# Reordering a fused gMLP, attention and PEER block: exponentials, scaling, weight splits and gathers

## The chip, the core and the metric

The kernel runs on one core of a Trainium2 chip. The metric is the device time of one execution in microseconds (us), from runs that were timed on the chip. TensorE is called PE below, VectorE DVE, ScalarE ACT, GpSimd POOL and SyncE SP, as the profile does. POOL and SP and ACT also issue DMAs; each engine works through its own queue in order.

## What is computed

One layer of a streaming encoder, for 512 tokens of width 1024, all in float32:

```python
xn   = rms_norm(x, ln_mix_g);  proj = xn @ w_in            # 1024 x 2560
a    = gmlp_spatial_gating(proj[..., :512], proj[..., 512:1024], ...)
b    = banded_chunk_attention(q, k, v, ...)                # 8 heads of 64
x    = x + concat([a, b]) @ w_out
# PEER on y = rms_norm(x): 8 heads, 16 of 128 x 128 experts each
q    = y @ w_query;  sc = q . sub_keys                     # two halves of 128 keys per head
s_top, i_top = top_k(sc, 16)                               # per half
best, pos = top_k(all sums of the two halves, 16)          # 16 experts per head and token
g    = softmax(best)
h    = gelu(expert_u[eidx] . y)
out  = x + sum(g * h * expert_v[eidx])
```

There are 16384 experts, each with a row of 1024 in `expert_u` and in `expert_v`.

## The kernel before

**Two ways to the experts.** Of the four tiles of 128 tokens, three (and of these all tokens but the last 64 for the first product) are computed densely: all 16384 experts' products with the tokens, scaled with a matrix of gates that is zero for experts that were not chosen. The experts are cut into 128 blocks of 128 (`NB`), two blocks make a chunk c (`BC`, 64 chunks). The remaining tokens gather the chosen rows from memory by indirect DMAs of POOL.

**Split weights.** A float32 product is made of three products of a high and a low half: `load_split` loads 512 KB (`raw`, three buffers, issued by SP), ACT copies the high half (`hi`, L155, five buffers), and DVE or POOL subtracts it for the low half (`lo`, L156, five buffers). `mm3` (L194 to L196) multiplies hi by hi, hi by lo and lo by hi. In the first stage `load_pieces` does the same with lines L143 and L144; there a piece is split as a whole, but for the first piece, which comes in two DMAs and is split in two.

**The stages in time.** (1) Norm, the first product with `w_in`, attention and gate, up to about 245 us. (2) Routing of the three dense tiles (queries, keys, top 16) with some blocks of the first expert product filled in. (3) The gate stage, some 430 to 590 us, which builds the matrix of gates. (4) The second product over the chunks c, to the end.

**The gate stage** runs over n, eight tokens a step (48 steps and two more). Its order on PE, DVE, ACT and POOL is the program's order. In a step, POOL multiplies the one-hot digits `hb` and `lb` to `bm` (L968, three buffers), PE multiplies `bm` and `am` of step n - 2 to the gates (L985, sixteen instructions), ACT copies them out (L988), DVE makes `am` (L976, three buffers) and a row product of gathered rows (L665, `dots_early`), POOL issues one gather of a row of `expert_u` for 128 tokens and slots (L655, `gather_early`, six buffers), DVE makes digits for a later step, PE does a share of the first expert product (`multiply_some`, results in `pu`, two buffers, activated by ACT's gelu at L719), and one split of the next weights is put in the queues: `split_next`, on DVE, each fourth on POOL, while fewer than `HELD` = 2 tiles are ready.

**The second product**, chunk c: load and split two blocks of `expert_v`, scale the activations with the gates (`act` times `gc`, L1168 on DVE), take their high half (`wh`, L1169 on ACT) and low half (`wl`, L1170 on DVE), and multiply on PE (L1202). The gates `gc` come back from memory in groups of four chunks, in two buffers. As long as c + 25 < 64, the chunk is followed by two tiles of the first expert product for chunk c + 25, each with its gelu. Between these, DVE handles the gathered rows (L1128, L1139). Only PE's order is the program's here; the other queues are ordered by a planner, which weighs priorities and expected times, and an instruction is kept behind another one of the same engine where `tc.issue_after` or `queued_behind` says so. `done` holds the newest gelu, `marked` the newest `am` or `wl`.

For every third chunk (`ROUTE`) up to c = 21, `route_gathered` routes one head of the gathered tokens: top 16, candidates, choice, and the softmax with its exponential on ACT (L804), which stands between a subtraction (L803) and a sum (L806) on DVE. Exponential and gelu need different tables on ACT, so ACT_TABLE_LOAD instructions stand ahead of them.

Of the kernel before, what the change touches and what calls it, by code (L numbers as in the profile page):

```python
# [8 lines left out]
F32 = mybir.dt.float32  # L9
# [5 lines left out]
ALU = mybir.AluOpType  # L15
# [52 lines left out]
AHEAD = 25  # L68
LAST = 2
HELD = 2  # L70
SOME = 15
FILL = (0, 1, 2, 3, 4, 4, 3, 3)
DELAY = 6
# [20 lines left out]
def hybrid_block(tc, x, ln1, w_in, gng, wsT, bsb, qkg, bias, w_out, ln2, wq, skT, uT, ud, vd, out):  # L94
    nc = tc.nc
    ctx = ExitStack()
    with ctx:
# [35 lines left out]
        def load_pieces(src, n, b):  # L133

            raw, hi, lo = big("raw", F32, RAW), big("hi", F32R, HI), big("lo", F32R, LO)
            m = 1024 // n
            cs = [slice(i * m, (i + 1) * m) for i in range(n)]
            for i in range(n):
                nc.sync.dma_start(raw[:, cs[i]] if n > 1 else raw.rearrange("p (a b) -> p a b", b=b),
                                  src[:, i, :] if n > 1 else src)  # L140

            def split(i=0):
                nc.scalar.activation(hi[:, cs[i]], raw[:, cs[i]], AF.Copy)  # L143
                nc.vector.tensor_tensor(lo[:, cs[i]], raw[:, cs[i]], hi[:, cs[i]].bitcast(F32), op=ALU.subtract)  # L144
            return [v.rearrange("p (a b) -> p a b", b=b) for v in (hi, lo)], split

        def load_split(src, eng=nc.vector, **dims):
# [29 lines left out]
        class Pieces:  # L177
# [5 lines left out]
                self.parts[j] = load_pieces(self.w[2 * j * P:2 * (j + 1) * P, self.c * CW:(self.c + 1) * CW]  # L183
                                            .rearrange("(k p) n -> p k n", p=P), 1 if j else self.first, CW)

            def split(self, j, i=0):
                self.parts[j][1](i)

            def __call__(self, k, cols=slice(0, CW)):
                return tuple(v[:, k % 2, cols] for v in self.parts[k // 2][0])  # L190
# [83 lines left out]
        with tc.tile_pool(name="prea", bufs=1, reuse_waits="tile") as prea:  # L274
# [33 lines left out]
            def scale_of(t):  # L308
                r = rs1[:, t:t + 1]
                nc.vector.tensor_scalar(r, r, 1.0 / D, EPS, op0=ALU.mult, op1=ALU.add)  # L310
                nc.scalar.activation(r, r, AF.Sqrt)
                return nc.vector.reciprocal(r, r)
# [6 lines left out]
            with tc.manual_schedule(engines=first):  # L319
# [17 lines left out]
                def product(t, ps, ks):  # L337
                    tok = slice(t * P, (t + 1) * P)
                    for k in ks:
                        mm3(ps, (xh[:, k, tok], xl[:, k, tok]), w_at(k), k == 0, k == KT - 1)  # L340
# [2 lines left out]
                halves(0, 1, xg[1])  # L343
                w_at.split(0, 1)
                product(0, ps0, range(2))
                w_at.split(1)
                product(0, ps0, range(2, 4))
                scale_of(0)
                w_at.load(3)
                w_at.split(2)  # L350
                product(0, ps0, range(4, 6))
                pss = turned(1)
                w_at.split(3)

                def next_halves(t, pss):
                    xg = [gained(ps, j) for j, ps in enumerate(pss)]
# [439 lines left out]
                                          mask[:, i, :, :, None].to_broadcast([P, n, TOPK, m]), other)  # L796
            nc.vector.tensor_copy(to, tree[:, :, :, 0])

        def softmax(pool, best, n):

            full = [P, n, TOPK]
            ex = pool.tile(full, F32, name="ex")
            nc.vector.tensor_tensor(ex, best, best[:, :, 0:1].to_broadcast(full), op=ALU.subtract)  # L803
            nc.scalar.activation(ex, ex, AF.Exp)  # L804
            zs = pool.tile([P, n], F32, name="zs")
            nc.vector.reduce_sum(zs, ex, axis=AX.X)  # L806
            nc.vector.reciprocal(zs, zs)
            nc.vector.tensor_tensor(best, ex, zs[:, :, None].to_broadcast(full), op=ALU.mult)
# [207 lines left out]
        with tc.manual_schedule(engines=engines):  # L1016
# [5 lines left out]
            for n in range(steps + LEAD):  # L1022
# [16 lines left out]
                    ready_early(NH - 3 + n)  # L1039
                if n:  # L1040
                    dots_early(LAGE, 1)
                if 1 < n < own - 7 and n % 4 != 1:
                    gather_early(1, gat, ROWA)
                if t + 1 < ND:
                    if c == per - 5:
# [26 lines left out]
                left = (AHEAD - LAST) * BC * KT - split * KT + made  # L1072
                some = -(-left // (steps + LEAD - n))
                multiply_some(some)
                if n > 1 and split < (AHEAD - LAST) * BC + HELD and len(ready) < HELD:
                    split_next(nc.vector if split % 4 else nc.gpsimd)
            while ready or open_tile:
                if split == AHEAD * BC and not weights:
# [28 lines left out]
        def route_gathered(b):  # L1107

            n = NH // PARTS
            sc = (scores.pop(b) if b in scores else scores_of(b, nc.sync))[0]  # L1110
            top, pos = keys(ep, n)
            for h in range(n):
                for p2 in range(2):
                    best_keys(ep, top, pos, h, p2, sc[:, h, p2, :])
            hs = slice(b * n * TOPK, (b + 1) * n * TOPK)
            best, to = (x[:, 0, hs].rearrange("p (h k) -> p h k", k=TOPK) for x in (gate, eidx))
            mask = ep.tile([P, 6 * n * TOPK], U32, name="mask", tag="mask", bufs=1)
            tree = ep.tile([P, D], F32, name="tree", tag="row", bufs=ROW)
            choose(ep, pairs(ep, top, pos, n, behind=list(routed if b else done)), n, best, to, mask,
                   tree[:, 0:n * TOPK * 32].rearrange("p (h k m) -> p h k m", h=n, k=TOPK))  # L1120
            softmax(ep, best, n)
            nc.vector.tensor_copy(eint[:, hs], eidx[:, 0, hs])

        def gather_u(j):
            row = ep.tile([P, D], F32, name="row", tag="row", bufs=ROW)
# [32 lines left out]
        def second_product(c, between):  # L1158
# [2 lines left out]
            act = acts.pop(c)  # L1161
            wh = ep.tile([P, BC, NDT], F32R, name="wh", tag="wh", bufs=2)
            wl = ep.tile([P, BC, NDT], F32R, name="wl", tag="wl", bufs=2)
            with queued_behind(marked if c < GB // BC else []):
                for b in range(BC):
                    bb = (c * BC + b) % GB
                    av = act[:, b, :].rearrange("p (n t) -> p n t", t=TG)
                    nc.vector.tensor_tensor(av, av, gc[:, 0:NDU // TG, bb, :], op=ALU.mult)  # L1168
# [46 lines left out]
        with tc.manual_schedule(engines={mybir.EngineType.PE}):  # L1215
            for c in range(NCHK):
# [7 lines left out]
                    if c:  # L1224
                        ahead()
                if c % ROUTE == 0 and c < PARTS * ROUTE:
                    route_gathered(c // ROUTE)
                passed = c + 1 + min(c + 1, NCHK - AHEAD)
                with tc.issue_after(mark.ins if hasattr(mark, "ins") else mark):
                    gather_some(min(total, total * max(0, passed - DELAY) // (weight - SLACK - DELAY))  # L1230
# [55 lines left out]
```

## Time and profile before

| | |
|---|---|
| time, median of 3 runs | 1425.32 us (1420.27 to 1426.73) |
| the profiled execution's own time | 1418.47 us |
| its span, first to last instruction | 1416.7 us |
| mean granted clock of PE | 0.998 |
| PE busy | 1387.3 us, 98% of the span |
| DVE busy | 1157.5 us, 82% |
| POOL busy | 699.0 us, 49% |
| ACT busy | 610.5 us, 43% |
| HBM traffic | 363.34 MB read, 31.46 MB written |

A row of a timeline gives start, duration, engine, line, operation, tiles (out <- in) and shapes; in brackets stands the time that the engine was idle before it and what ended that. A row of the waits gives the total, the number of waits and the longest. A row of the windows gives the stretch and its length, busy time of PE, its weight load, DVE, ACT and POOL with the number of instructions, then the granted clock, the DMA engines' share and GB/s. Busy shares are means over stages with different limits, so the waits of the engine that is nearly always busy are read place by place.

### The profile page before, as it was taken

The page shows a single profiled execution, that of the slowest core. Times are in us where ns is not written, and L with a number is a line of the kernel's source. Part 1 is how long each engine was busy: PE and PEld are TensorE (multiplying, and loading weights), DVE is VectorE, ACT ScalarE, POOL GpSimd, SP SyncE. Part 2 cuts the span into 40 slices and gives each one's busy share as a digit, 9 for nine tenths or more (in the row PEclk, how much of TensorE's full clock was granted, in tenths as well). Part 3 has the DMA queues.
Part 4 walks back from the last instruction along what each step waited for, and adds up shares of the span by engine and source line. Part 5 has one row for each costly group of instructions (what it writes and reads, how often), then busy time and mean ns, then how long its engine had stood idle before and what let it go on. Part 6 is the DMA issues. An engine that isn't in the chain of part 4 may idle for free.

```text
span 1416.7 us, 21660 instructions
## 1 busy us (share of the span) xinstructions
PE 1387.3 (98%) x7838; PEld 1224.6 (86%) x7838; DVE 1157.5 (82%) x2505; ACT 610.5 (43%) x955; POOL 699.0 (49%) x486
## 2 busy tenths in 40 slices
PE   9999999999998999989999999999999999999998
PEld 7887788899998989978998889889889989888877
DVE  5537845898999998679999999889989887688883
ACT  5447635443443545444434443334433334333331
POOL 0002104778779898325554556455565553345430
PEclk9999999999999999999999999999999999999999
DMA  4452326667667999978999899999999998888882
GB/s 165 133 193 75 105 75 193 209 214 275 235 229 257 330 352 272 292 265 332 334 331 356 328 352 347 355 376 353 386 375 365 347 364 311 288 332 326 335 335 89
DMA packets 164330, 396.24 MB, mean 280 GB/s; under 512 B 12880, under 2 KB 75232, under 8 KB 162176
## 3 DMA queue, kind: packets, MB, share of 16 engines
q1 hardware_dynamic: 64640, 194.14, 37.9%
q0 software_dynamic: 48176, 173.46, 33.2%
q10 hardware_dynamic: 51408, 27.27, 6.5%
q8 instruction: 61, 1.00, 0.3%
q14 instruction: 45, 0.37, 0.1%
HBM read 363.34 MB, written 31.46 MB: 279 GB/s over the span
## 4 chain that ended last, share of the span: by engine, by line
PE 31%; DVE 12%; DMA 8%; issue 4%; ACT 1%; POOL 0%; SPq 0%; DVEq 0%; ACTq 0%; POOLq 0%
PE pa L1202 13%; PE px L1202 6%; PE pu L194 4%; PE pu L196 4%; PE pu L195 4%; DMA gc<-gd 4%; DVE lo L156 3%; DVE row L1128 2%; DVE acc L1139 2%; DMA row<-in_ud,eint 2%; DVE act L1168 1%; DMA raw<-in_uT 1%; DMA row<-in_vd,eint 1%; DVE wl L1170 1%; DMA raw<-in_vd 1%
## 5 line engine op out<-in xcount | busy, mean ns | idle before, releaser
L155 ACT ACTIVATE hi<-raw 128x1024 fp32r<-128x1024 f32 x296 | 312.9, 1059 | 470.9 <-DMA raw<-in_vd 156.6
L156 DVE TENSOR_TENSOR lo<-raw,hi 128x1024 fp32r<-128x1024 f32 x244 | 307.0, 1259 | 72.1 <-ACT hi L155 71.6
L1126 POOL DMA_INDIRECT row<-in_ud,eint x128 | 198.5, 1551 | 159.6 <-DVE acc L1139 107.2
L1137 POOL DMA_INDIRECT row<-in_vd,eint x128 | 179.7, 1404 | 192.0 <-DVE row L1128 131.5
L194 PE MATMUL pu<-xch,hi 128*128 128x320 f32 x784 | 247.5, 316 | 8.6 <-ACT act L719 8.6
L196 PE MATMUL pu<-xch,lo 128*128 128x320 f32 x784 | 242.8, 310 | 0.0
L195 PE MATMUL pu<-xcl,hi 128*128 128x320 f32 x784 | 242.7, 310 | 0.0
L1202 PE MATMUL pa<-lo,wh 128*128 128x512 f32 x512 | 199.7, 390 | 0.0
L1202 PE MATMUL pa<-hi,wh 128*128 128x512 f32 x512 | 199.4, 389 | 0.0
L156 POOL TENSOR_TENSOR lo<-raw,hi 128x1024 fp32r<-128x1024 f32 x52 | 124.1, 2401 | 116.3 <-ACT hi L155 115.3
L1139 DVE SCALAR_TENSOR_TENSOR acc<-row,hw,acc 128x1024 f32<-128x1024 f32 x128 | 165.6, 1294 | 2.4 <-DMA row<-in_vd,eint 2.0
L1128 DVE SCALAR_TENSOR_TENSOR row<-row,xb 128x1024 f32<-128x1024 f32 x128 | 155.9, 1220 | 12.0 <-DMA row<-in_ud,eint 12.0
L1202 PE MATMUL pa<-hi,wl 128*128 128x512 f32 x512 | 158.4, 389 | 0.0
L194 PEld LDWEIGHTS pu<-xch,hi 128*128 128x128 f32 x784 | 148.0, 189 | 12.0 <-ACT act L719 10.4
L195 PEld LDWEIGHTS pu<-xcl,hi 128*128 128x128 f32 x784 | 148.1, 189 | 1.4
L196 PEld LDWEIGHTS pu<-xch,lo 128*128 128x128 f32 x784 | 147.8, 188 | 0.2 <-DVE lo L156 0.2
L1202 PEld LDWEIGHTS pa<-hi,wh 128*128 128x128 f32 x512 | 96.1, 188 | 20.6
L1202 PEld LDWEIGHTS pa<-hi,wl 128*128 128x128 f32 x512 | 96.1, 188 | 20.2
L1202 PEld LDWEIGHTS pa<-lo,wh 128*128 128x128 f32 x512 | 96.1, 188 | 20.2
L985 PE MATMUL pa<-bm,am 128*128 128x128 f32 x768 | 96.3, 279 | 7.9 <-DVE am L976 5.0
L985 PEld LDWEIGHTS pa<-bm,am 128*128 128x128 f32 x768 | 92.3, 194 | 10.8 <-issue 5.5
L1202 PE MATMUL px<-hi,wh 128*128 128x512 f32 x256 | 100.1, 391 | 0.6 <-ACT hi L155 0.6
(236 smaller groups left out, 2634.1 us busy)
## 6 DMA issues: line engine op xcount, KB each, us to landing
raw<-in_uT SPq DMA_DIRECT2D x128, 512.0 KB, 5.6
raw<-in_vd SPq DMA_DIRECT2D x128, 512.0 KB, 6.1
gd<-gst ACTq DMA_DIRECT2D x24, 1024.0 KB, 8.9
gc<-gd SPq DMA_DIRECT2D x15, 1280.0 KB, 9.8
raw<-in_w_in SPq DMA_DIRECT2D x19, 512.0 KB, 4.6
raw<-in_wq SPq DMA_DIRECT2D x16, 512.0 KB, 4.5
raw<-in_w_out SPq DMA_DIRECT2D x8, 512.0 KB, 3.7
gc<-gd SPq DMA_DIRECT2D x15, 256.0 KB, 10.3
```

What stands on the lines that cost most here:

```text
L155: top = nc.scalar.activation(hi, raw, AF.Copy)
L156: ins = eng.tensor_tensor(lo, raw, hi.bitcast(F32), op=ALU.subtract)
L194: nc.tensor.matmul(ps, lh[0], rh[0], start=first, stop=False)
L195: nc.tensor.matmul(ps, lh[0], rh[1], start=False, stop=False)
L196: nc.tensor.matmul(ps, lh[1], rh[0], start=False, stop=last)
L985: nc.tensor.matmul(ps[:, i * P:(i + 1) * P], am[:, 4 * q + i, :], bm[:, 4 * q + i, :], start=True, stop=True)
L1126: nc.gpsimd.indirect_dma_start(out=row, out_offset=None, in_=ud, in_offset=bass.IndirectOffsetOnAxis(ap=eint[:, j:j + 1], axis=0))
L1128: nc.vector.scalar_tensor_tensor(row, row, 1.0, xb0, op0=ALU.mult, op1=ALU.mult, accum_out=hw[:, j:j + 1])
L1137: nc.gpsimd.indirect_dma_start(out=row, out_offset=None, in_=vd, in_offset=bass.IndirectOffsetOnAxis(ap=eint[:, j:j + 1], axis=0))
L1139: nc.vector.scalar_tensor_tensor(acc0, row, hw[:, j:j + 1], acc0, op0=ALU.mult, op1=ALU.add)
L1168: nc.vector.tensor_tensor(av, av, gc[:, 0:NDU // TG, bb, :], op=ALU.mult)
L1202: nc.tensor.matmul(accs[t][half], (wh, wh, wl)[k][:, b, tok], w[b][k % 2][:, ds_], start=first and k == 0, stop=last and k == 2)
```

## The change

Four things are reordered; no arithmetic is added or taken away.

- **Loop exponentials behind gelus.** `softmax` is cut in two. `route_gathered` ends with the subtraction (`shifted`) and returns; exponential, sum, reciprocal and product follow two chunks later (c = 2, 5, 8, ...), the exponential behind the newest gelu on ACT.
- **Scaling behind weights.** The scaling products (L1168) of every chunk are queued behind the newest `wl` on DVE, where that held for the first four chunks alone.
- **The gate stage's begin.** Up to n = 8 (`EASY`) a split is put in the queues only at even n. Gathers are issued from n = 6 on, but for n = 9, 17 and 25; before it was from n = 2 on, but for n = 5, 9, 13, ..., 29.
- **First weights by halves.** Pieces 1, 2 and 3 of the first weights are split in two halves each, and the scale of the first tile of tokens comes behind the split of piece 2, not ahead of it.

```diff
+EASY = 8
...
-            def split(i=0):
-                nc.scalar.activation(hi[:, cs[i]], raw[:, cs[i]], AF.Copy)
-                nc.vector.tensor_tensor(lo[:, cs[i]], raw[:, cs[i]], hi[:, cs[i]].bitcast(F32), op=ALU.subtract)
+            def split(i, n):
+                c = slice(i * (1024 // n), (i + 1) * (1024 // n))
+                nc.scalar.activation(hi[:, c], raw[:, c], AF.Copy)
+                nc.vector.tensor_tensor(lo[:, c], raw[:, c], hi[:, c].bitcast(F32), op=ALU.subtract)
...
-                w_at.split(1)
+                w_at.split(1, 0)
+                w_at.split(1, 1)
                 product(0, ps0, range(2, 4))
+                w_at.load(3)
+                w_at.split(2, 0)
+                w_at.split(2, 1)
                 scale_of(0)
-                w_at.load(3)
-                w_at.split(2)
                 product(0, ps0, range(4, 6))
                 pss = turned(1)
-                w_at.split(3)
+                w_at.split(3, 0)
+                w_at.split(3, 1)
...
-        def softmax(pool, best, n):
+        def shifted(pool, best, n):
 
             full = [P, n, TOPK]
             ex = pool.tile(full, F32, name="ex")
             nc.vector.tensor_tensor(ex, best, best[:, :, 0:1].to_broadcast(full), op=ALU.subtract)
-            nc.scalar.activation(ex, ex, AF.Exp)
+            return ex
+
+        def softmax(pool, best, n, ex=None, behind=()):
+
+            full = [P, n, TOPK]
+            if ex is None:
+                ex = shifted(pool, best, n)
+            with queued_behind(behind):
+                nc.scalar.activation(ex, ex, AF.Exp)
...
-                if 1 < n < own - 7 and n % 4 != 1:
+                if EASY - 3 < n < own - 7 and n % 8 != 1:
                     gather_early(1, gat, ROWA)
...
-                if n > 1 and split < (AHEAD - LAST) * BC + HELD and len(ready) < HELD:
+                if n > 1 and split < (AHEAD - LAST) * BC + HELD and len(ready) < HELD and (n > EASY or n % 2 == 0):
                     split_next(nc.vector if split % 4 else nc.gpsimd)
...
-            softmax(ep, best, n)
             nc.vector.tensor_copy(eint[:, hs], eidx[:, 0, hs])
+            return best, n, shifted(ep, best, n)
...
-            with queued_behind(marked if c < GB // BC else []):
+            with queued_behind(marked):
...
-                    route_gathered(c // ROUTE)
+                    chosen = route_gathered(c // ROUTE)
+                if c % ROUTE == ROUTE - 1 and c < PARTS * ROUTE:
+                    softmax(ep, *chosen, behind=list(done))
```

More of the change, by code (lines that the diff above doesn't have):

```diff
@@ L184, in load, with split @@
                                             .rearrange("(k p) n -> p k n", p=P), 1 if j else self.first, CW)
-            def split(self, j, i=0):
-                self.parts[j][1](i)
+            def split(self, j, i=0, n=2):
+                self.parts[j][1](i, n)
             def __call__(self, k, cols=slice(0, CW)):
```

## The prediction

> **What bounds the kernel now.** I read the page's engine list first, then the waits of TensorE (PE), then the windows with the granted clock, then the timelines around each wait. Times below are microseconds from the start of the span; n is a step of the gate stage, c a chunk of the second product.
>
> ```profile
> PE 1387.3 (98%) x7838; PEld 1224.6 (86%) x7838; DVE 1157.5 (82%) x2505; ACT 610.5 (43%) x955; POOL 699.0 (49%) x486
> ```
>
> PE is busy for 98% of the span, so nothing off PE counts unless PE waits for it. The waits are a short list (total, times, longest):
>
> ```profile
> PE pu L194 <- ACT act L719: 9.7, 6, 4.7
> PE pa L985 <- DVE am L976: 5.0, 2, 4.7
> PE pa L985 <- POOL bm L968: 2.8, 8, 1.1
> PE px L1202 <- DVE wl L1170: 1.6, 1, 1.6
> PE pu L195 <- DVE lo L144: 1.3, 3, 0.8
> ```
>
> The four parts of the change aim at these rows in this order: exponentials at the first, the gate stage at the second and third, scaling at the fourth, first weights at the fifth. Together they hold 20.4. Two single waits of 4.7 cost more than they show: in the windows behind them the granted clock (first number after the five engines) is 0.66.
>
> ```profile
> 458.00:463.00 5.00, 4.71 (x25) 4.74 (x26) 4.97 (x10) 1.17 (x2) 3.23 (x3) 0.66 1.00 352
> ...
> 632.00:637.00 5.00, 5.00 (x25) 5.00 (x25) 1.04 (x1) 0.00 (x0) 1.32 (x2) 0.66 0.99 408
> ```
>
> A third of 5.0 is 1.7 lost each time. So 20.4 + 3.4 = 23.8 is the most that this change can bring.
>
> **Part 1, exponentials behind gelus (-7).** ScalarE (ACT) works its queue in order. Before, the routing of a head puts its exponential (L804) wherever the planner finds it ready; the gelu (L719) that empties an accumulator of the first product stands behind it, and PE waits for that accumulator.
>
> ```profile
> 627.81 0.21 ACT L804 ACTIVATE ex<-ex 128x16 f32<-128x16 f32 x1 [3.15 <-DVE ex L803]
> 627.93 1.99 ACT L155 ACTIVATE hi<-raw 128x1024 fp32r<-128x1024 f32 x2
> 629.94 1.28 ACT L719 ACT_TABLE_LOAD   x1
> 631.23 0.77 ACT L719 ACTIVATE act<-pu 128x320 f32<-128x320 f32 x2
> ```
>
> ```profile
> 631.72 0.41 PE L194 MATMUL pu<-xch,hi 128*128 128x320 f32 x1 [4.71 <-ACT act L719]
> ```
>
> ```profile
> 752.91 0.42 PE L194 MATMUL pu<-xch,hi 128*128 128x320 f32 x1 [0.78 <-ACT act L719]
> ```
>
> ```profile
> 800.07 0.41 PE L194 MATMUL pu<-xch,hi 128*128 128x320 f32 x1 [0.92 <-ACT act L719]
> ```
>
> ```profile
> 848.25 0.41 PE L194 MATMUL pu<-xch,hi 128*128 128x320 f32 x1 [2.13 <-ACT act L719]
> ```
>
> ```profile
> 797.10 0.22 ACT L804 ACTIVATE ex<-ex 128x16 f32<-128x16 f32 x1 [4.19 <-DVE ex L803]
> ```
>
> ```profile
> 846.46 1.28 ACT L719 ACT_TABLE_LOAD   x1
> ```
>
> After it, the subtraction (L803) stays in the routing at c = 0, 3, 6, ... and the exponential is queued two chunks later, behind the gelu just issued: its input is long there, and the longest stretch to the next gelu follows. At 631 the wait for DVE, the exponential and one table load, 3.15 + 0.21 + 1.28 = 4.64, leave the queue ahead of the gelu; of 4.71 nearly nothing stays, and the 1.7 of slow clock go too: 6.3. At 752 a load is 1.28 against a wait of 0.78, at 800 the 4.19 alone exceed 0.92: both go, 1.7. At 848 only the reload, 1.28, stands right before the gelu: 1.3 of 2.13 go. Sum 9.3. Against it: the table is still reloaded ahead of the next gelu, eight times 1.28. Eight exponentials gave four waits in their bad place, and no more than one in five should be caught in the new one: 1.6 x 1.28 = 2.0. I take -7; ends: the four waits and the clock, -10.2, and +3 if the reloads are caught where VectorE (DVE) is late (next rival).
>
> The Trainium skill, page "ScalarE: Activation LUTs", section "What ACT_TABLE_LOAD costs", puts a switch of table sets at about 2.66, a load and as much again to drain. The trace disagrees in these rows: 629.94 + 1.28 is 631.22, and the gelu starts at 631.23. By the page's figure two caught reloads would cost 4 and this part would bring 5.
>
> **Part 2, scaling behind weights (-1.6).** From c = 4 on, the products act x gc (L1168) were free to go ahead of the weights' low halves (L1170) of earlier chunks. DVE then stood idle until the gates had landed:
>
> ```profile
> DVE act L1168 <- DMA gc<-gd: 40.3, 12, 5.3
> ```
>
> ```profile
> 1349.71 2.10 DVE L1168 TENSOR_TENSOR act<-act,gc 128x320 f32<-128x320 f32 x5 [5.31 <-DMA gc<-gd]
> ```
>
> Only once did that reach PE: the 1.6 for L1170 in the list above, right behind this row. Queued behind the wl of the chunk before, L1168 comes about a chunk before its use; its two products take 2 x 0.42 = 0.84 (2.10 / 5), so wl of the same chunk is not late. Behind the waiting L1168 stood everything on DVE, gathers' row work included; that is freed, but PE has no other wait there. Ends: -1.8 and +0.5. Late next: nothing on PE until the end.
>
> **Part 3, the gate stage (0).** Up to n = 8 the splits of weights come at even n alone, and gathers start at n = 6 and skip n = 9, 17, 25, where they started at n = 2 and skipped 5, 9, 13, ..., 29. The stall removed:
>
> ```profile
> 451.95 5.07 DVE L156 TENSOR_TENSOR lo<-raw,hi 128x1024 fp32r<-128x1024 f32 x1
> ```
>
> ```profile
> 451.68 2.38 POOL L156 TENSOR_TENSOR lo<-raw,hi 128x1024 fp32r<-128x1024 f32 x1
> 454.02 1.91 POOL L968 TENSOR_TENSOR bm<-hb,lb 128x1024 f32<-128x1024 f32 x1
> ```
>
> ```profile
> 458.29 3.59 PE L985 MATMUL pa<-bm,am 128*128 128x128 f32 x16 [4.74 <-DVE am L976]
> ```
>
> A lo on DVE that mostly takes 1.22 took 5.07: it ended 1.1 after POOL's back-to-back lo and bm had ended at 455.93. The Trainium skill, page "SBUF — State Buffer", section "Who interferes with whom", states that a DVE instruction with two SBUF inputs and a GpSimd one that reads SBUF exclude each other, whoever starts first. The trace agrees, 5.07 against 1.22. It also speaks against this change: bm after bm with no gather between them is just what a lo has to sit out.
>
> With splits at n = 2, 4, 6, 8 the lo of n = 5 is gone from this place and the stall with its clock, 4.74 + 1.7 = 6.4, should go. What comes instead: at n = 2 the lo started beside a gather and held up bm of n = 3 (2.67 long); without the gather that bm starts 1.0 earlier and comes first:
>
> ```profile
> 441.66 1.23 DVE L156 TENSOR_TENSOR lo<-raw,hi 128x1024 fp32r<-128x1024 f32 x1 [1.14 <-ACT hi L155]
> ```
>
> ```profile
> 440.93 1.02 POOL L655 DMA_INDIRECT rowe<-in_ud,eui  x1 [0.27 <-POOL eui L671]
> 442.01 2.67 POOL L968 TENSOR_TENSOR bm<-hb,lb 128x1024 f32<-128x1024 f32 x1
> ```
>
> so this lo waits about 1.0 (or 3.0, should the next bm get in as well), and PE needs it at once. PE's tiles don't run out otherwise: a step takes three of a tile's eight k there, so a split every 2.7 steps is enough. A split's hi on ACT and the next load on SP, which waits for its raw buffer, move along with it. Then POOL. Its ledger to 536.65:
>
> ```profile
> L968 POOL TENSOR_TENSOR bm<-hb,lb 128x1024 f32<-128x1024 f32 x33 | 65.5, 1993 | 5.4 <-DVE lb L957 4.3 <-PE pa L985 0.6
> L655 POOL DMA_INDIRECT rowe<-in_ud,eui x22 | 25.7, 1169 | 3.6 <-issue 2.7 <-POOL eui L671 0.3 <-PE pa L985 0.2
> ```
>
> ```profile
> 433.20:536.65 103.45, 96.98 (x755) 94.44 (x754) 100.11 (x148) 50.36 (x83) 95.44 (x61) 0.98 0.96 311
> ```
>
> ```profile
> 504.20 2.05 PE L985 MATMUL pa<-bm,am 128*128 128x128 f32 x16 [0.17 <-POOL bm L968]
> ...
> 507.31 2.05 PE L985 MATMUL pa<-bm,am 128*128 128x128 f32 x16 [0.18 <-POOL bm L968]
> ```
>
> ```profile
> 539.42 1.95 PE L985 MATMUL pa<-bm,am 128*128 128x128 f32 x16
> 542.09 1.95 PE L985 MATMUL pa<-bm,am 128*128 128x128 f32 x16
> ```
>
> POOL is at work for 95.44 of 103.45. With gathers a step takes 507.31 - 504.20 = 3.11, POOL's pace; without, 2.67, PE's own. The same 22 gathers are issued, now in n = 6 to 30: three move from n = 2, 3, 4, where the buffers of bm (three) leave POOL time, to n = 13, 21, 29, where it sets the pace. Each costs (25.7 + 3.6) / 22 = 1.33: 4.0. POOL's lo (2.38) moves from n = 5, inside the stall, to n = 8. So -6.4 + 1.0 + 4.0 + 2.4 = +1.0; a part of the time won at n = 7 does help POOL too, and I take 0. DVE's rows move with the gathers and are hidden under POOL's pace. Ends: -5.4 (POOL keeps up) and +2.9.
>
> **Part 4, first weights by halves (-0.3).**
>
> ```profile
> 13.36 1.06 ACT L143 ACTIVATE hi<-raw 128x1024 fp32r<-128x1024 f32 x1 [1.54 <-DMA raw<-in_w_in]
> ```
>
> ```profile
> 14.45 1.23 DVE L144 TENSOR_TENSOR lo<-raw,hi 128x1024 fp32r<-128x1024 f32 x1 [1.37 <-ACT hi L143]
> ```
>
> ```profile
> 7.43 0.68 DVE L144 TENSOR_TENSOR lo<-raw,hi 128x512 fp32r<-128x512 f32 x1
> ```
>
> The first lo of a piece is there half a split earlier (1.23 - 0.68 = 0.55 on DVE, about 0.5 of the 1.06 on ACT), and part of the 1.3 that PE waits goes. But the last piece waits for its DMA until 13.36 in either kernel; by halves its lo start 0.5 sooner and take 2 x 0.68 - 1.23 = 0.13 more, so the work for the next tile of tokens behind them is 0.3 to 0.4 earlier. The scale moved behind the split is used only after the whole product, and on SP the loads keep their order. Ends: -1.3 and +0.4.
>
> **Sum.** -7 - 1.6 + 0 - 0.3 = -8.9. The profiled execution took 1418.47 (span 1416.7), so 1409.6; the median of the three runs is 6.85 higher, 1425.32, and 1416.4 is the forecast for a median.
>
> **The rivals.**
>
> *POOL keeps up.* The gate stage keeps most of its 6.4. For it: 8 of 103.45 idle on POOL. Against: 6.4 of its work (4.0 + 2.4) lands where PE waits for it. Then -8.9 - 5 = -13.9: 1411.4.
>
> *The loop's gain comes back as new waits.* Between 640 and 850 DVE is at work for 202.61 of 210:
>
> ```profile
> 640.00:850.00 210.00, 206.16 (x1128) 184.98 (x1127) 202.61 (x468) 94.08 (x139) 113.16 (x78) 1.00 0.91 338
> ```
>
> PE's waits there are 0.78 + 0.92 + 2.13 = 3.83, and DVE has 7.4 free; if lateness on DVE and not the exponential holds the gelus, the three waits return in other places, and of the first one (6.4 with its clock) some half goes. Then -3 - 1.6 - 0.3 = -4.9: 1420.4, no change that can be told. For it: 96% on DVE, and 848, where the exponential stood ahead of a wait for DMA. Against: the 4.19 and 3.15 are the exponentials' own.
>
> *Slower: DVE waits for a late exponential.* The sum (L806) follows the exponential on DVE, whose queue is in order. Behind the gelu, the exponential is as late as PE and ACT are; if the planner puts L806 close behind, DVE stands, and with 7.4 free in 210, eight waits w cost PE 8w less about 7. From w = 2 it decides: 16 - 7 = 9 lost; the 7 of part 1 are lost too. Then -8.9 + 7 + 9 = +7.1: 1432.4. For it: the 12 waits of L1168 show that DVE does stand in such places. Against: L806 has no urgency and can stand anywhere within three chunks.
>
> **How the numbers follow.** My sum 0.45, POOL keeps up 0.15, gain comes back 0.28, slower 0.12. A measurement tells about 0.5%, 7.1. My sum lies 1.8 beyond that and is within some 4 either way: of its 0.45, 0.30 are faster and 0.15 the same. With 0.15 and a little of the third: faster 0.48, same 0.40 (0.15 + 0.25), slower 0.12. The range reaches from POOL keeping up with 2.4 of the 3.2 that part 1 can bring beyond -7 (1411.4 - 2.4 = 1409.0) to 1428, short of the slower case; my own sum alone 1412 to 1421.
>
> **What would show it.** Right: no wait for L719 over 1 between 600 and 860, each L804 right behind an L719; the waits of L1168 for gc near 0; no clock of 0.66 behind 458 or 632; steps of 3.1 in the gate stage from about n = 10 to n = 30, with PE waiting for bm. Wrong: gelus still late with nothing but hi ahead of them, DVE idle before L806, a new gap at n = 3, or gate steps of 2.8 under gathers.

## The result, and the profile after

The changed kernel takes 1411.62 us (median of 7 runs, 1410.74 to 1413.98), the kernel before, in the same sessions, 1419.00 (7 runs, 1416.26 to 1426.73). The ratio is 0.9934 with a 95% interval of 0.9916 to 0.9951: faster by 0.5 to 0.8%. The profiled execution took 1410.74, with a span of 1409.0, against 1418.47 and 1416.7.

The busy line and the first waits of PE after, then the one wait for `gc` that is left on DVE (total, times, longest):

```profile
PE 1386.7 (98%) x7838; PEld 1224.6 (87%) x7838; DVE 1154.3 (82%) x2508; ACT 612.0 (43%) x960; POOL 673.0 (48%) x486
```

```profile
PE pa L998 <- POOL bm L981: 4.2, 8, 1.2
PE pu L196 <- ACT act L724: 3.0, 3, 2.0
PE pa L998 <- DVE ff L889: 1.9, 2, 1.5
PE pa L998 <- DVE am L989: 1.7, 2, 1.4
```

```profile
DVE act L1181 <- DMA gc<-gd: 4.5, 1, 4.5
```

Lines have moved by 2 to 13: L719 is L724 now, L985 is L998, L968 is L981, L1168 is L1181. The wait for the gelu fell from 9.7 to 3.0, that for `am` from 5.0 to 1.7; that for `bm` rose from 2.8 to 4.2, and `ff` came in new. The wait for `wl` is gone.

**The loop.** The timeline of ACT around the longest wait that is left, PE's row for it, and two windows behind (the first number after the five engines is the granted clock):

```profile
627.18 2.00 ACT L157 ACTIVATE hi<-raw 128x1024 fp32r<-128x1024 f32 x2 [1.83 <-issue]
629.09 0.74 ACT L724 ACTIVATE act<-pu 128x320 f32<-128x320 f32 x2
```

```profile
629.56 0.41 PE L196 MATMUL pu<-xch,hi 128*128 128x320 f32 x1 [2.02 <-ACT act L724]
...
765.93 0.42 PE L196 MATMUL pu<-xch,hi 128*128 128x320 f32 x1 [0.73 <-ACT act L724]
```

```profile
458.00:463.00 5.00, 5.00 (x44) 5.00 (x43) 4.97 (x9) 2.75 (x5) 4.17 (x3) 1.00 0.96 280
...
631.00:634.50 3.50, 3.50 (x15) 3.50 (x15) 1.32 (x2) 0.00 (x0) 3.10 (x2) 0.51 0.98 413
```

No exponential and no table load stands ahead of this gelu any more, and still PE waits 2.02: two `hi`'s stand there, and the first began at 627.18, after 1.83 of idle time for which the profile names no releaser. The slow clock behind it has stayed, 0.49 x 3.5 = 1.7. At 752, 800 and 848 PE waits no longer; 0.73 at 766 is new.

**The gate stage.** The clock behind 458 is full, the stall is gone, and the stage is not shorter. The starts of the first and the last step's products, before and after:

```profile
438.10 1.95 PE L985 MATMUL pa<-bm,am 128*128 128x128 f32 x16
...
581.81 1.95 PE L985 MATMUL pa<-bm,am 128*128 128x128 f32 x16
```

```profile
438.62 1.95 PE L998 MATMUL pa<-bm,am 128*128 128x128 f32 x16
...
582.53 1.95 PE L998 MATMUL pa<-bm,am 128*128 128x128 f32 x16
```

581.81 - 438.10 = 143.71 before, 582.53 - 438.62 = 143.91 after. What was won at 458 went in five waits, two of them for POOL's `bm` and three for DVE:

```profile
444.31 0.42 PE L198 MATMUL pu<-xch,lo 128*128 128x320 f32 x1 [0.78 <-DVE lo L158]
...
487.30 0.35 PE L998 MATMUL pa<-bm,am 128*128 128x128 f32 x1 [1.40 <-DVE am L989]
...
499.47 0.38 PE L998 MATMUL pa<-bm,am 128*128 128x128 f32 x1 [1.20 <-POOL bm L981]
512.68 0.38 PE L998 MATMUL pa<-bm,am 128*128 128x128 f32 x1 [0.99 <-POOL bm L981]
526.02 0.35 PE L998 MATMUL pa<-bm,am 128*128 128x128 f32 x1 [1.54 <-DVE ff L889]
```

A step of 3.11 does not tell by itself whose pace it is. Before, the products that start at 466.15 and 469.26 have nine matmuls of the first product between them and no wait, so 3.11 is PE's own pace there. Those at 504.20 and 507.31 have six and a wait for `bm`. After the change PE's rows wait for `bm` from 499.47 to 518.89 and once more at 549.99; only there does POOL set the pace.

### The profile page after: what moved, and what is told of

It reads as the page before. It is cut to its first block, busy times and chain, and to the rows that moved or that the text cites. A ratio compares the mean times of both kernels' runs of the same rounds, so it can differ in the third digit from the quotient of the medians.

```text
span 1409.0 us, 21692 instructions
## 1 busy us (share of the span) xinstructions
PE 1386.7 (98%) x7838; PEld 1224.6 (87%) x7838; DVE 1154.3 (82%) x2508; ACT 612.0 (43%) x960; POOL 673.0 (48%) x486
## 4 chain that ended last, share of the span: by engine, by line
PE 78%; DVE 13%; DMA 2%; POOL 2%; issue 2%; ACT 2%; ACTq 0%; DVEq 0%; POOLq 0%
PE pa L1215 23%; PE px L1215 12%; PE pu L196 9%; PE pu L198 9%; PE pu L197 9%; PE pa L998 3%; PE pa L196 3%; PE pa L197 3%; PE pa L198 3%; DVE rowe L670 2%; DVE lo L158 2%; DVE tree L800 1%; DVE am L989 1%; DMA raw<-in_vd 1%; POOL rowe L660 1%
## 5 line engine op out<-in xcount | busy, mean ns | idle before, releaser
L1139 POOL DMA_INDIRECT row<-in_ud,eint x128 | 193.0, 1508 | 180.8 <-DVE acc L1152 129.4
L1150 POOL DMA_INDIRECT row<-in_vd,eint x128 | 159.7, 1247 | 178.0 <-DVE row L1141 118.6
L998 PE MATMUL pa<-bm,am 128*128 128x128 f32 x768 | 95.1, 277 | 8.0 <-POOL bm L981 4.2
L998 PEld LDWEIGHTS pa<-bm,am 128*128 128x128 f32 x768 | 90.7, 191 | 11.7 <-POOL bm L981 6.5
```

The source lines that it names most:

```text
L998: nc.tensor.matmul(ps[:, i * P:(i + 1) * P], am[:, 4 * q + i, :], bm[:, 4 * q + i, :], start=True, stop=True)
L1139: nc.gpsimd.indirect_dma_start(out=row, out_offset=None, in_=ud, in_offset=bass.IndirectOffsetOnAxis(ap=eint[:, j:j + 1], axis=0))
L1150: nc.gpsimd.indirect_dma_start(out=row, out_offset=None, in_=vd, in_offset=bass.IndirectOffsetOnAxis(ap=eint[:, j:j + 1], axis=0))
```

## The experiments

All were timed beside the kernel before, whose medians in the four sessions were 1420.2 to 1421.2; the ratio of the whole change is from another session. One per mille is 1.4 us. Every ratio is to the kernel before.

### The four parts, each by itself

The first theory was that the parts add up, as the sum in the prediction does.

**Exponentials alone.**

```diff
-            softmax(ep, best, n)
+            return best, n, shifted(ep, best, n)
...
+                if c % ROUTE == ROUTE - 1 and c < PARTS * ROUTE:
+                    softmax(ep, *chosen, behind=list(done))
```

> The kernel before with the exponentials behind the gelus alone. My theory: this part carries most of the gain. The trace of the changed kernel lost 2.02 + 1.7 (clock) at 629 where the one before lost 4.71 + 1.7, and 0.73 in place of 0.78 + 0.92 + 2.13 between 750 and 850, so this kernel is 5 to 6 faster, about 0.9960, and the waits for am at 458 and for wl at 1356 stay as they were. Rival: DVE's lateness held the gelus; then the waits for L719 come back in other places and the time is the same within 2. Rival: the gain is the scaling's; then likewise.

Measured: 1422.68, ratio 1.0014 (1.0002 to 1.0025). The theory fell; the first rival, by which the waits come back in other places, held. The wait at 631 did shrink, to 2.30, but a new one came, with DVE and ACT ahead of it as follows:

```profile
723.46 0.63 PE L194 MATMUL pu<-xch,hi 128*128 128x320 f32 x1 [3.37 <-ACT act L719]
```

```profile
713.03 1.70 DVE L1176 TENSOR_TENSOR act<-act,gc 128x320 f32<-128x320 f32 x4 [1.96 <-DMA gc<-gd]
714.65 1.22 DVE L156 TENSOR_TENSOR lo<-raw,hi 128x1024 fp32r<-128x1024 f32 x1
715.78 1.69 DVE L1176 TENSOR_TENSOR act<-act,gc 128x320 f32<-128x320 f32 x4
```

```profile
720.61 1.06 ACT L155 ACTIVATE hi<-raw 128x1024 fp32r<-128x1024 f32 x1 [1.50 <-DMA raw<-in_uT]
721.68 1.28 ACT L719 ACT_TABLE_LOAD   x1
722.97 0.44 ACT L719 ACTIVATE act<-pu 128x320 f32<-128x320 f32 x1
```

The gelu stood behind a `hi` whose load was late, and behind the table's reload. What made the load late is not shown. DVE stood 1.96 for `gc` and then did eight products in a batch, but the load that this `hi` waits for had been issued ahead of that, at 709.61, as an earlier `lo` ended (708.36 + 1.22). The kernel before has the same wait for `gc` (1.56, at 710.58) and no wait of PE behind it. With both edits of the loop the same load was issued at 707.82 and the `hi` began at 716.89; the reload at 717.97 then cost PE nothing.

**Scaling alone.**

```diff
-            with queued_behind(marked if c < GB // BC else []):
+            with queued_behind(marked):
```

> The kernel before with the scaling queued behind the weights in all chunks, alone. My theory: DVE's 40 of waiting for gates go, but only the 1.64 at 1356 was PE's, so it is 1.5 to 2 faster, about 0.9988, and the waits for gelus at 631, 752, 800 and 848 stay. Rival: DVE freed of these waits is what lets the gelus come in time; then 3 to 5 faster, and the waits at 752 to 848 shrink without any exponential being moved.

Measured: 1418.67, 0.9984 (0.9972 to 0.9996). The wait for `wl` at 1356 is gone, as are those at 752, 800 and 848, with the exponentials unmoved. But at 632 a wait of 3.45 is left, and another one is new:

```profile
632.04 0.63 PE L194 MATMUL pu<-xch,hi 128*128 128x320 f32 x1 [3.45 <-ACT act L719]
...
786.97 0.42 PE L194 MATMUL pu<-xch,hi 128*128 128x320 f32 x1 [2.07 <-ACT act L719]
```

On ACT a load and an exponential stand at 781.36, between two `hi`'s, and the gelu's reload at 785.18, right before the gelu. The time is a little better than the theory's 0.9988, but three waits that it said would stay are gone: in this the rival was right, though not in its 3 to 5 us.

**Gate stage alone.**

```diff
-                if 1 < n < own - 7 and n % 4 != 1:
+                if EASY - 3 < n < own - 7 and n % 8 != 1:
...
-... and len(ready) < HELD:
+... and len(ready) < HELD and (n > EASY or n % 2 == 0):
```

> The kernel before with the gate stage's spread splits and later gathers, alone. My theory: POOL sets the stage's pace, so the front stall (4.74 and 1.7 of clock) goes and is given back by n = 34: the last gate products start 0.5 to 1 later than before, and the time is the same within 1.5 (0.999 to 1.001). Rival: the stall that is removed stays removed, 4 to 6 faster, about 0.9965.

Measured: 1422.27, 1.0008 (0.9996 to 1.0021): nothing, as the prediction's 0 had it.

**First weights alone.** The edit is the one in `load_pieces` and in the order of the first product.

> The kernel before with the first weights split by halves, alone. My theory: -0.3, which a measurement can't tell from nothing; in the trace PE's waits before 20 shrink from about 2.3 to 1.5 when they are counted from the first weight's arrival. Rival: the smaller instructions cost more than they bring, as the changed kernel's first 25 held 0.2 more lost time than before; then 0 to +0.5.

Measured: 1421.04, 1.0002 (0.9991 to 1.0012): nothing. PE's waits up to 25 us for `lo`, `hi` and `rs` or `xh` went from 1.3 + 0.7 + 0.3 to 0.8 + 0.4 + 0.4.

The four ratios differ from 1 by +1.4, -1.6, +0.8 and +0.2 per mille, in sum +0.8; the whole change gives -6.6. So two parts must work on each other.

### The loop: both parts together, and without the table loads

> Before with the loop's exponentials queued behind the gelus and all scalings queued behind the weights; the gate stage and the first weights stay as before. Alone the two gave 1.0014 and 0.9984, a sum of -0.3. Theory 'the two only pay together': the exponentials leave the gelus' way and, with no wait for gc on DVE, no batch of late scalings holds the raw buffers, so the new wait at 723 (3.37) of the exponentials alone and that at 787 (2.07) of the scaling alone are both absent; PE's waits for the gelu between 600 and 900 fall from 8.5 to under 3.5, and the ratio is 0.9945 to 0.996 (-8 to -6). Rival 'the parts add up': ratio 0.9985 to 1.0005, with one of the two new waits still there. Rival 'the gain came from the gate stage, by what it hands on to the loop': ratio near 1, with waits for the gelu of 6 or more.

Measured, with both edits of the loop and nothing else: 1413.97, 0.9948 (0.9934 to 0.9961). The waits at 723 and 787 are absent, 2.30 at 630 and 1.19 at 767 are left. The theory that the two only pay together held.

Next, the exponential as a copy in its old place; only the table loads are missing then.

```diff
-        def softmax(pool, best, n):
+        def softmax(pool, best, n, f=AF.Exp):
...
-            nc.scalar.activation(ex, ex, AF.Exp)
+            nc.scalar.activation(ex, ex, f)
...
-            softmax(ep, best, n)
+            softmax(ep, best, n, AF.Copy)
```

The last of these lines is the loop's; the other softmax keeps its exponential.

With the scaling behind the weights:

> The scalings queued behind the weights, the exponential left in its old place in the loop but turned into a copy (so the loop's softmax weights lack the exponential): ACT's queue, waits and buffers are as with the scaling alone (0.9984), only the table switches, 16 loads of 1.28, are gone. Theory 'place, not price': the wait of the copy for DVE's subtraction still holds the gelu near 632; what stays of the 3.45 there is 2 to 2.3, and the wait at 787 (2.07, two loads ahead of it) goes; ratio 0.9955 to 0.997. Rival 'the table loads are the whole price': no wait for the gelu over 0.5 between 600 and 900, ratio 0.9945 or below. Rival 'DVE holds the gelus whatever ACT does': waits of 5 or more stay there, ratio 0.998 or more.

Measured: 1413.03, 0.9944 (0.9930 to 0.9957), the same as with the exponentials moved. It lies at the edge between the theory and the rival, and the trace decides for the rival in most places. Later copies waited on ACT for DVE as long as the exponentials had done, with no wait of PE over 0.5 behind the three waits of 4.05, 6.19 and 3.22; the longest:

```profile
793.23 0.22 ACT L804 ACTIVATE ex<-ex 128x16 f32<-128x16 f32 x1 [6.19 <-DVE ex L803]
```

The wait of 2.30 at 629 stayed, though, and one of 0.97 at 770 behind a late load of `raw`, so the loads weren't all. The planner put the second head's copy behind the gelu here, at 629.60, so the place has changed at this one spot as well.

With the scalings free, as before:

> Before with the loop's exponential left in its old place and turned into a copy (the loop's softmax weights lack the exponential), and the scalings left free as before. With the scalings behind the weights this gave 0.9944, the exponentials alone gave 1.0014 and both edits 0.9948. Theory 'the table loads are the price, and DVE held up by gc costs as much once more in another place': the 16 loads of 1.28 are gone, the first wait near 630 falls to 2.3, but a late batch of scalings still holds raw buffers, so one or more waits of 1 to 3 for the gelu stay or turn up between 700 and 850, and the wait for the weights' low half at 1356 (1.6) stays; ratio 0.997 to 0.9995. Rival 'the loads are the whole price, whatever DVE does': waits for the gelu between 700 and 900 under 1 in all, ratio 0.9945 to 0.9965.

Measured: 1419.55, 0.9998 (0.9986 to 1.0009), a little above the theory's range, and the first wait is 3.59, not the 2.3 that the theory had. DVE waits for `gc` 40.6 in all, and PE:

```profile
629.99 0.64 PE L194 MATMUL pu<-xch,hi 128*128 128x320 f32 x1 [3.59 <-ACT act L719]
...
795.12 0.50 PE L1202 MATMUL px<-lo,wh 128*128 128x512 f32 x1 [1.39 <-DVE lo L156]
...
847.20 0.41 PE L194 MATMUL pu<-xch,hi 128*128 128x320 f32 x1 [1.31 <-ACT act L719]
```

So taking the loads off ACT is worth nothing that can be told while the scalings are free, by this route as by the other. The table sums, for one execution of each, PE's single waits over 0.5 between 600 and 1380, and the time lost to a slow clock there (each window of 5 us by 1 less its granted clock, those below 0.97; some of these windows hold time in which PE stood, so this is an upper bound):

| kernel | ratio | waits | slow clock | sum |
|---|---|---|---|---|
| before | 1 | 4.71 + 0.78 + 0.92 + 2.13 + 1.6 = 10.1 | 1.8 | 11.9 |
| exponentials moved | 1.0014 | 2.30 + 3.37 + 0.73 + 0.67 + 0.56 + 2.08 = 9.7 | 5.0 | 14.7 |
| exponentials as copies | 0.9998 | 3.59 + 0.57 + 1.39 + 0.57 + 1.31 + 0.89 = 8.3 | 1.7 | 10.0 |
| scaling behind | 0.9984 | 3.45 + 0.60 + 2.07 = 6.1 | 5.1 | 11.2 |
| scaling behind, exponentials moved | 0.9948 | 2.30 + 1.19 = 3.5 | 1.7 | 5.2 |
| scaling behind, exponentials as copies | 0.9944 | 2.30 + 0.97 = 3.3 | 1.7 | 5.0 |
| the whole change | 0.9934 | 2.02 + 0.73 = 2.8 | 1.7 | 4.5 |

The sums stand in the order of the ratios but for the fourth row, whose execution lost 5.1 to the clock. Both edits bring 6.7 here and 5.2 per mille, 7.4, in time. A part of the interplay is the clock: each part alone leaves waits of over 2, and a wait of that length mostly brings a window at half clock.

The rows also take apart the 4.71 at 631, from one execution of each kernel: 2.30 stays whatever is done to loads and exponentials, the loads are 3.45 - 2.30 = 1.15, the exponential that waits for a late DVE 3.59 - 2.30 = 1.29; 4.74 in sum.

**What holds the other 2.30?** With both edits of the loop and the spread splits of the gate stage, the `hi`'s of the loop's first chunks were queued behind an earlier gelu (`gelus` is the list of the gelus so far):

```diff
-                if j >= PRE:
-                    split_tile(j, eng)
+                with queued_behind(gelus[-3:-2] if AHEAD <= j // BC < AHEAD + 4 else []):
+                    if j >= PRE: split_tile(j, eng)
```

> Both edits of the loop and the spread splits (0.9925), and in the loop's first chunks (four chunks of weights of the first product) the split of a tile is queued behind the gelu three tiles back, so that no two hi's stand on ACT ahead of a gelu that PE waits for. The rest of the wait for the gelu near 626 (2.30, with a window of half clock behind it of 1.7) is there put down to two hi's ahead of the gelus, the first of which waits 2.27 for its buffer. Theory 'order on ACT': that wait goes below 0.5 with its slow clock, -3 to -4, ratio 0.990 to 0.9905. Rival 'buffers': the hi buffer is what PE's tiles need, the same wait comes back as a wait for hi or lo of 1 or more near 626; ratio 0.992 to 0.9935.

Measured: 1411.41, 0.9938 (0.9919 to 0.9956), no better than 0.9925 without it. The rival held; instead of 2.30 behind the gelu, 2.05 + 2.30 are lost to halves that the tiles lack:

```profile
622.38 0.41 PE L194 MATMUL pu<-xch,hi 128*128 128x320 f32 x1 [2.05 <-ACT hi L155]
...
625.33 0.64 PE L196 MATMUL pu<-xch,lo 128*128 128x320 f32 x1 [2.30 <-DVE lo L156]
```

**Is the reload at 763 a price?** Behind each moved exponential a gelu of one element per partition was set, so that the gelu's table is back at once:

```diff
-                nc.scalar.activation(ex, ex, AF.Exp)
+                ins = nc.scalar.activation(ex, ex, AF.Exp)
+            if behind:
+                back = pool.tile([P, 1], F32, name="back")
+                with queued_behind([getattr(ins, "ins", ins)]):
+                    nc.scalar.activation(back, ex[:, 0, 0:1], AF.Gelu_apprx_tanh)
```

> Both edits of the loop and the spread splits (0.9925); behind each moved exponential a gelu of one element per partition stands on ACT, which brings the gelu table back at once, so that the reload (1.28) no longer stands in front of the next gelu that PE may wait for. Theory 'one reload is still caught, at 763': the wait of 1.29 there goes, the one near 626 (2.30, two hi's ahead, no load) stays; -1.2, ratio 0.991 to 0.992. Rival 'DVE and the buffers hold the gelu, the reload only fills their wait': the wait near 763 stays above 0.8, ratio 0.992 to 0.9935.

Measured: 1410.03, 0.9926 (0.9910 to 0.9942), against 0.9925 without it. PE's wait moved by one tile and stayed as long. Without the small gelu, ACT and PE:

```profile
760.88 1.28 ACT L719 ACT_TABLE_LOAD   x1
762.18 0.44 ACT L719 ACTIVATE act<-pu 128x320 f32<-128x320 f32 x1
765.26 1.06 ACT L155 ACTIVATE hi<-raw 128x1024 fp32r<-128x1024 f32 x1 [2.64 <-DMA raw<-in_vd]
```

```profile
762.67 0.41 PE L194 MATMUL pu<-xch,hi 128*128 128x320 f32 x1 [1.29 <-ACT act L719]
```

and with it:

```profile
765.07 1.06 ACT L155 ACTIVATE hi<-raw 128x1024 fp32r<-128x1024 f32 x1 [3.69 <-DMA raw<-in_vd]
766.03 0.42 ACT L719 ACTIVATE act<-pu 128x320 f32<-128x320 f32 x1
```

```profile
766.50 0.41 PE L194 MATMUL pu<-xch,hi 128*128 128x320 f32 x1 [1.25 <-ACT act L719]
```

The next tile's `hi` waits for its load of `raw` in both kernels, until 765.26 and 765.07. That load is what is late there; the reload only filled its wait.

### The gate stage, part by part

The two edits of the gate stage were put, one at a time, on the kernel with both edits of the loop.

> The loop's two edits and the spread splits of the gate stage; gathers as before, from n = 2. Against the loop's two edits alone it tells what the spread splits do by themselves. The prediction's terms: stall and clock -6.4, lo behind bm +1.0, POOL's lo moved +2.4, no gathers moved: -3.0, that is 0.002 under the loop alone. Theory now 'POOL takes back what is won ahead of it': with gathers from n = 2 POOL is at work all the time from the front on, so the stage's end moves by only -1 to 0 (0.999 to 1.000 of the loop alone). Rival: a new wait of am or bm of 2 or more turns up near n = 5 to 8 since DVE's and POOL's lo still meet there: +1 to +3.

Measured, spread splits: 1409.56, 0.9925 (0.9911 to 0.9938), 2.3 per mille or 3.3 us under the loop alone, though the two intervals overlap a little; my theory of the moment, -1 to 0, fell. The -3.0 that I expected counts the `lo` behind `bm`, +1.0, wrongly: the prediction has it from the gather that is missing at n = 2, and this kernel still issues that one. By the prediction's own terms the spread splits alone are -6.4 + 2.4 = -4.0. From the first to the last step it is 578.66 - 437.62 = 141.04, against 144.30 with the loop alone:

```profile
437.62 1.95 PE L993 MATMUL pa<-bm,am 128*128 128x128 f32 x16
...
578.66 1.95 PE L993 MATMUL pa<-bm,am 128*128 128x128 f32 x16
```

A part of these 3.3 is the clock of one execution: behind the stall, the step took 5.59 with the loop alone and 4.76 in the kernel before. Against the stage before, 143.71, the spread splits bring 2.7.

> The loop's two edits and the later gathers (from n = 6, skipping n = 9, 17, 25); splits as before, two at a time. By the prediction's ledger three gathers of 1.33 move to where POOL sets the pace: +4.0, if the stall at 458 stays whole; with POOL free of gathers around the stall the bm's are ahead and the stall (4.74) shrinks to some 2 to 3 with its slow clock gone: -2 to -4. Sum 0 to +2, 1.000 to 1.0015 of the loop alone. If the stall stays whole with its clock: +4, 1.003.

Measured, later gathers: 1411.50, 0.9934 (0.9920 to 0.9948). The stall at 458 is gone by this edit alone: POOL, with no gather to issue, runs ahead and stands 3.30 for PE before its own `lo` at 452.73, and DVE's `lo`'s at 446.41 and 449.53 take 1.22 each. But waits of 1.71, 0.98 and 1.53 follow from 498 to 526, and the stage is 143.37 long. The times of this kernel and of the loop alone overlap. I had expected 2 to 3 of the stall to stay; nothing of it did.

So either edit removes the stall, and a stall is removed once. With both, the stage takes 143.91; with the splits alone 141.04. The later gathers, on top of the splits, cost 2.87, of which 0.78 is the wait for `lo` at 444.31 that the splits alone do not have. The kernel with the spread splits and without the later gathers, 0.9925, has a lower ratio than the changed kernel's 0.9934, but their intervals overlap; that it is faster is shown by the two traces alone (span 1405.9 against 1409.0).

**Fewer gathers in the stage.** `EARLY = 7` for 6, on the kernel with the spread splits:

> Both edits of the loop and the spread splits (0.9925), and seven gathers per head instead of six issued in the routing stage ahead of the gate stage, so that six or so of the gate stage's 22 are gone from POOL there. By the ledger a gather costs POOL 1.33 and POOL sets the pace (steps of 3.11 with gathers, 2.67 without): 6 x 0.44 = 2.6 at PE's own pace to 6 x 1.33 = 8; theory 'POOL sets the pace of the gate stage': the stage is 3 to 6 shorter than 142.7 from its first to its last product, ratio 0.9885 to 0.991. Rival 'the gathers are only moved to where POOL or their row buffers hold something else': the gain comes back in the routing stage ahead as waits, ratio 0.992 to 0.994.

Measured: 1409.67, 0.9923 (0.9905 to 0.9941). The gate stage is 579.70 - 441.02 = 138.68, that is 2.36 shorter, with 19 gathers on POOL between 430 and 590 instead of 22: not six fewer, as I had expected, but three, at 0.79 each. And the stage starts 3.4 later, with a new wait at its front door:

```profile
429.26 0.42 PE L194 MATMUL pu<-xch,hi 128*128 128x320 f32 x1 [2.21 <-ACT act L719]
```

The rival held: the work is only moved.

## Why the prediction came out as it did

The forecast was -8.9 from the kernel before and 1416.4; measured is -7.4 by the medians, -9.4 by the ratio (its interval is -7.0 to -11.9), and 1411.62. The level is lower than the forecast's since it was built on a median of three, 1425.32, and the seven runs have 1419.00. The forecast's own statement that the profiled execution would take 1409.6 stands against 1410.74. Of the prediction's own signs of being wrong, "gelus still late with nothing but hi ahead of them" came, at 629, and a new gap near n = 3, 0.78.

**Part 1 (-7): near in size, wrong in how.** The step that failed is that "3.15 + 0.21 + 1.28 = 4.64, leave the queue ahead of the gelu; of 4.71 nearly nothing stays, and the 1.7 of slow clock go too: 6.3". 4.71 went to 2.02 and the clock stayed: 2.7. I read ACT's idle time before the exponential, 3.15, as time that the gelu lost. Most of it would have passed in any case. PE ran out of work at 631.72 - 4.71 = 627.01 before and at 629.56 - 2.02 = 627.54 after; the first of the two `hi`'s began 0.92 behind that point before and 0.36 ahead of it after. So the late exponential cost 1.28 and the table load another 1.28, together 2.56 of the 2.69 that went. An idle time on ACT is a price only as far as what stands behind is ready. In the same way 4.19 at 797 was no price by itself: with the loads gone and the scaling behind, 6.19 in that place cost nothing. The waits at 752, 800 and 848, forecast at 3.0, gave 3.83 - 0.73 = 3.1, but that size is right by luck: with the scaling alone and no exponential moved they are gone as well. The 2.0 for reloads caught later were not drawn in that size: one wait of 0.73 is there, and in a kernel close to this one the small gelu showed a wait of that kind to be a late load. So 9.3 - 2.0 became 2.7 + 3.1 = 5.8.

**And it isn't part 1's alone.** The sum gave part 1 -7 and part 2 -1.6, each on its own. Measured alone they are +2.0 and -2.3 (0.0014 and 0.0016 of 1420), together -7.4. That their sum came out is luck, too: neither part stands alone. My sentence "PE has no other wait there" on the rows behind L1168's wait is the step that failed in part 2: the free scalings cost PE more than that one wait. It was the rival "the loop's gain comes back as new waits" that the exponentials alone ran into; with both edits it did not come. By which path the free scalings reach PE stays open. I took it to be DVE standing for `gc`, by way of `lo`, `raw` and `hi`. But of the 40.3 only 4.06 + 1.56 + 0.61 = 6.2 lie between 600 and 860, where PE waited for gelus, and the load behind the wait at 723 was issued ahead of the wait for `gc` there.

**Part 2 (-1.6): its own place right.** L1170's wait of 1.6 is gone, the waits of L1168 fell from 40.3 to 4.5, and nothing at the end took their place.

**Part 3 (0): right in sum, its terms too large.** Alone 1.0008; in the trace 143.71 became 143.91. By the prediction's terms the splits are -6.4 + 2.4 = -4.0 and the later gathers 1.0 + 4.0 = +5.0; measured are -2.7 (-3.3 against the loop alone) and +2.87. Both are too large, in opposite senses, so the sum holds. The `lo` behind `bm` at n = 2 was put at +1.0 and is 0.78, from a `lo` that took 2.08 beside two `bm`'s; the gathers themselves, put at +4.0, cost about 2.1. No wait shows the +2.4 for POOL's `lo` by itself. One of the prediction's signs, steps of 3.1 from about n = 10 on, could not tell: 3.11 is PE's own pace there. The Trainium skill, page "SBUF — State Buffer", section "Who interferes with whom", by which a DVE instruction with two inputs in SBUF and a GpSimd one that reads SBUF exclude each other, agrees with 2.08 against 1.22 here.

**Part 4 (-0.3): too small to see.** Alone, 1.0002 tells nothing. In the trace PE's waits fell by 0.7, while the last piece's `hi` began 0.4 later in that execution (13.76 against 13.36).

**The rivals.** "POOL keeps up" did not come: PE waits for `bm` from 499.47 to 518.89, and the stage is as long as before. "DVE waits for a late exponential" did not come: after the change DVE waited 0.9 in all for the exponentials. On the reload, the Trainium skill's 2.66 for a switch of tables (page "ScalarE: Activation LUTs", section "What ACT_TABLE_LOAD costs") again isn't what the rows have: 760.88 + 1.28 is 762.16, and the gelu starts at 762.18.

## What to carry to other kernels

An engine's idle time before an instruction is its price only if what stands behind it is ready; look up what the next instruction itself waits for before you count it. When two parts of a change act on queues that feed each other (here the scalings on DVE and the exponentials on ACT, which both stand ahead of the `lo` and `hi` that PE needs), their gains need not add: run them alone and together. A stall between two engines is removed once, by either side, and a second cure only leaves its costs.

## What the runs showed of the hardware

A wait of PE of 2 us or more is mostly followed by some 3.4 us at half clock, about 1.7 lost, at times more. It is not the same in every execution: a wait of 2.30 near 626 to 630 brought it in most kernels, and none in the kernel with fewer gathers and in the one with the small gelu; the 2.13 at 848 in the kernel before and the 2.21 at 429 with fewer gathers brought none either. The stall of 4.7 at 458 stands in seven kernels, and the step behind it took 4.76 to 5.81 against 3.11: 1.7 to 2.7 lost. The windows of the kernel with the small gelu:

```profile
627.00:632.00 5.00, 4.87 (x30) 4.66 (x31) 2.61 (x4) 0.40 (x2) 3.75 (x4) 1.00 0.99 390
632.00:637.00 5.00, 5.00 (x24) 4.12 (x23) 2.14 (x7) 1.25 (x3) 0.94 (x1) 1.00 1.03 419
```

With the scaling alone, a wait of 3.45 in that place cost seven:

```profile
631.00:638.00 7.00, 5.96 (x22) 5.96 (x23) 2.58 (x6) 2.80 (x5) 3.33 (x3) 0.51 1.01 406
```

Here the clock is at about half for all of the 7, and PE stands for 1.04 of them, so up to 0.49 x 5.96 = 2.9 is lost behind one wait. Waits of 1.71 and less brought no slow clock. The Trainium skill, page "TensorE: Matmul & The Clock Gate", section "HAM oscillation — how this bites in real kernels", warns of idle gaps over about 3.4 us; here 2.02 did it. The Trainium skill, same page, section "Part 1: The HAM clock gate (the "warmup" mystery)", has the clock judged over windows of that length that run freely. The waits of 2.13 to 2.30 without a slow clock would fit that, but no run here shows it.

The issue of a gather on POOL also takes longer beside DVE. Of the 22 in the kernel before, 17 took 0.98 to 1.02 and five took 1.79 (at 447.97, 456.09, 486.86, 509.29 and 521.29); in each of these five a `lo` had begun on DVE ahead of the issue and ran beside its first 0.93. Where a `lo` began during the issue (440.93, 444.83, 477.08 and 533.30) it took no longer.
